# Bin results stacked in the rows of one tile, and sums sent back to tokens as a high and a low part in one product

## Chip, cores and metric

One Trainium2 chip, one core (core 0). The metric is the device time of one launch in microseconds (us); lower is better. The engines are named as the profile names them: PE (TensorE) multiplies, PEld loads its weights, DVE (VectorE), ACT (ScalarE), POOL (GpSimd), and SP, which here only issues the DMA transfers of the weight stream.

## What is computed

The reference runs 256 tokens of width 1024 through two stacked blocks. Only the two mixtures of experts matter here:

```
# first mixture: 8 experts, 1024 -> 2816 -> 1024, two experts per token
logits = ht @ router
top_vals, top_idx = lax.top_k(logits, 2)
gates = softmax(top_vals)
out = sum_e gate[:, e] * ((silu(ht @ wg[e]) * (ht @ wu[e])) @ wd[e])

# second mixture: 4 groups of 4 experts, 1024 -> 256 -> 1024,
# one group per token, two experts inside it
g_val, g_idx = lax.top_k(softmax(ht @ w_rg + b_rg), 1)
hid = silu(a) * u * combine[..., None]
out = einsum('tef,efd->td', hid, w_down)
```

With the inputs given, the router of the reference sends 25, 63, 73, 46, 66, 88, 87 and 64 tokens to the eight experts of the first mixture, and 62, 47, 92 and 55 tokens to the four groups of the second.

## The kernel before

All weights come as one stream of 1 MB chunks, read once and in order; SP issues the transfers (lines 163 and 171) as soon as one of 11 buffers comes free, five of them called raw, six of them pairs called whi and wlo. A buffer comes free when the unit of work that used it is done (`retire`). In the mixtures nothing else is loaded, so each stretch goes at the pace of the stream or at the pace of PE, whichever is slower there, with a reserve of a few chunks between them.

An expert (in the second mixture a group) works on a **bin** of up to 96 token slots. The tokens of a bin are picked by a product with a one-hot matrix (`one_hots`, `gather`). The first 64 slots are computed always. The other 32 are computed inside `tc.If(more == 1)`, a branch on PE that is taken where a bin has more than 64 tokens. More than 96 would go to a fallback (`overflow`), behind a branch of all engines after the third expert of each mixture; it isn't entered here.

Per expert the units of work come in this order: gate-up of a group of columns (`bin_unit`), the down product of the group before (`bin_down`), the turning of the newest hidden values (`turn_hid`, which calls `bin_hid`), the next gate-up, and so on. The first mixture has six groups per expert (five of 512 columns, one of 256), so six hidden values are turned per expert; the second has one unit per expert.

- `bin_unit` puts gate and up of the 64 slots side by side into two halves of the rows of one PSUM bank (64 weight columns of PE each, both products at once), and those of the 32 slots into the four quarters of a second bank.
- `bin_mul` (lines 988 to 999) makes silu(gate) * up by three ACT and three DVE instructions. Its result tile `h` holds the 64 slots in rows 64 to 127 and the 32 slots in rows 32 to 63, in other columns.
- `bin_hid` (lines 1001 to 1009) transposes `h` on PE: for each 128 columns one transpose of 64 rows (line 1005) and one of 32 (line 1007); ACT copies the result for the down product (line 1008).
- `bin_down` sums the down products of an expert or group over its units in two PSUM banks `dn`.
- `bin_y` (lines 1029 to 1035) copies the two banks to SBUF in float32: two ACT copies (1032, 1034) and one DVE copy (1033). It runs 12 times, once per expert of the first mixture and once per group of the second.
- `scatter` (lines 1037 to 1054) sends the sums back to the tokens, once per half of the tokens, inside the gate-up of a later unit. Two float32 products of 64 rows each (line 1042, called through `mm`, so at line 342 in the profile) go to two banks, and inside a branch (line 1043) four more of 64 rows and 256 columns (line 1047). DVE adds the banks to `x` (line 1052 or 1054).
- `one_hots_T` (lines 910 to 922) turns the one-hots for `scatter`: three batches of four products with the identity, each followed by an ACT copy (line 920). It runs six times, once per pair of bins.
- `last_down` (line 1079) ends each mixture: there `bin_y` and `scatter` come right behind the last down product, and the next block waits for `x`.

The order of the work is that in which this code is written; DVE and ACT take their instructions strictly in that order.

Of the kernel before, what the change touches and what calls it, by code (L numbers as in the profile page):

```python
# [18 lines left out]
P = 128  # L19
# [18 lines left out]
WIN = 288  # L38
W_A, W_B0, W_B1 = 0, 128, 160
# [205 lines left out]
def block_kernel(ctx: ExitStack, tc: tile.TileContext, stream, x_in, cst_in, cols_in, small_in, sgu_in,  # L245
# [651 lines left out]

# [12 lines left out]
    def one_hots_T(pm, p):  # L910


        got = []
        for tag, w in (("k3" if p % 2 == 0 else "sguT", W_A), (f"t{6 + p % 2}", W_B0), (f"t{4 + p % 2}", W_B1)):
# [4 lines left out]
            pt = sl(tag, [2, 2, P])  # L919
# [32 lines left out]
    def to_slots(pm, i, src, n):  # L952

        b = ps("ms")
        for j, w in enumerate((W_A, W_B1)):
            for tb in range(2):
                mm(b[:, j * n:(j + 1) * n], pm[:, tb, i, w:w + P].bitcast(F32), src(tb), tb == 0, tb == 1)
# [4 lines left out]
    def bin_unit(xT, more, n, hooks=()):  # L962
# [5 lines left out]
        for r in range(KT // kc):  # L968
            row = W.take()
            for j in range(kc):  # L970
                k, at = kc * r + j, 2 * n * j
                todo.append((k, row, at))
                for h in range(2):
                    mm(a[h * HALF:(h + 1) * HALF, 0:n], xT[:, k, 0:HALF], row[:, at + h * n:at + (h + 1) * n], k == 0,
# [3 lines left out]
        with tc.If(more == 1) as c:  # L978
            for k, row, at in todo:
                for q in range(4):  # L980
                    c0 = at + (q % 2) * n + (q // 2) * m
# [6 lines left out]
    def bin_mul(banks, n, s, h, up=None):  # L988


        m = n // 2
        for (j, c0, m, lo, w, to) in ((0, 0, n, 0, HALF, HALF), (1, n, m, 0, MORE, MORE), (1, n + m, m, HALF, MORE, MORE)):
            r = slice(lo + w, lo + 2 * w)
            t, v, b = s[r, c0:c0 + m], h[to:to + w, c0:c0 + m], banks[j]
            nc.scalar.activation(t, b[lo:lo + w, 0:m], AF.Silu)  # L995
            if up is None:
                nc.vector.tensor_mul(v, b[r, 0:m], t)  # L997
            else:
                nc.vector.scalar_tensor_tensor(v, b[r, 0:m], up[r, j], t, op0=ALU.mult, op1=ALU.mult)

    def bin_hid(h, n, hT):

        b = ps("ms")[:, 0:4 * CAP].rearrange("p (k s) -> p k s", k=4)
        for f in range(n // P):
            nc.tensor.transpose(b[:, f, 0:HALF], h[HALF:P, f * P:(f + 1) * P], ident[HALF:P, HALF:P])
        for f in range(n // P):
            nc.tensor.transpose(b[:, f, HALF:CAP], h[MORE:HALF, n + f * P:n + (f + 1) * P], ident[MORE:HALF, MORE:HALF])  # L1007
# [21 lines left out]
    def bin_y(dn):  # L1029

        y = sl("k2", [512 + T])
        nc.scalar.activation(y[0:HALF, 0:512], dn[0][0:HALF], AF.Copy)
        nc.vector.tensor_copy(y[HALF:P, 0:512], dn[0][HALF:P])
        nc.scalar.activation(y[:, 512:], dn[1][:, 0:T], AF.Copy)
        return y

    def scatter(pt, i, y, tb, more, gate=None, tag="ms"):

        bs = [ps(tag), ps(tag)]
        for h in range(2):  # L1040
            r = slice(h * HALF, (h + 1) * HALF)
            mm(bs[h], pt[0][r, i, tb], y[r, 0:512], True, True)
        with tc.If(more == 1):  # L1043
            for q in range(2):
                for h in range(2):
                    r = slice(h * HALF, (h + 1) * HALF)
# [704 lines left out]
```

## Time and profile before

| | |
|---|---|
| median of 3 runs (range) | 1530.71 us (1527.68 to 1533.65) |
| profiled execution | 1530.3 us |
| its span, first to last instruction | 1528.6 us |
| PE busy | 1467.3 us, 96% |
| DVE, ACT, POOL busy | 618.5, 507.1, 115.5 us |
| HBM read | 426.02 MB, 279 GB/s over the span |
| granted clock of PE, mean | 0.990 of full speed |

Times in views of the trace count from the start of the span. The first mixture runs from about 427 to 1137 us and the second from about 1340 to 1501 us. A busy PE is not the same as a PE at its peak: the ends of matmuls are modelled, so the distance between two starts says more than the length of one. The DMA share is that of the 16 DMA engines; it reads 1.02 where they never rest.

### The profile page before, as it was taken

Reading aid. Unit: us, or ns where it says so; the run is one execution under the profiler, and the core shown is the slowest. Engines: PE = TensorE matmul, PEld = TensorE weight load, DVE = VectorE, ACT = ScalarE, POOL = GpSimd, SP = SyncE. Lnnn points to the kernel's source line nnn. Section 1 sums busy time; section 2 is a strip of 40 time slices with the busy share of each in tenths; the row PEclk is TensorE's granted clock in tenths of the full one; section 3 lists DMA queues with packets and bytes.
Section 4 is the critical chain, followed back from the end, with each engine's and each line's share of the span. In section 5 each row is a group of like instructions: output and inputs, shape, how many; then the busy total and the mean of one; then the engine's idle time right before and its main releaser. Section 6 shows DMA issues by size and latency. Waiting matters only on the chain. (4 is left out here: it accounts for less than half of the span.)

```text
span 1528.6 us, 22736 instructions
## 1 busy us (share of the span) xinstructions
PE 1467.3 (96%) x9322; PEld 888.1 (58%) x9322; DVE 618.5 (40%) x1132; ACT 507.1 (33%) x856; POOL 115.5 (8%) x98
## 2 busy tenths in 40 slices
PE   7899999999999999989999999999989999999998
PEld 5778888877753334433444444444347888865546
DVE  6986666689621211112111110101147566732235
ACT  7645444485431111111111111111136554621134
POOL 4804000053000000000000000000002000000000
PEclk9999999999999999999999999999999999999999
DMA  8434455542499999999999978899984345388870
GB/s 324 158 117 172 170 185 217 187 163 79 161 353 414 416 412 414 414 395 366 416 413 391 385 306 340 319 368 388 406 325 150 126 165 200 138 337 299 334 273 28
DMA packets 84086, 429.03 MB, mean 281 GB/s; under 512 B 9328, under 2 KB 9840, under 8 KB 53488
## 3 DMA queue, kind: packets, MB, share of 16 engines
q1 hardware_dynamic: 83232, 425.01, 71.8%
q8 instruction: 101, 1.65, 0.4%
q10 hardware_dynamic: 720, 2.10, 0.3%
q14 instruction: 33, 0.27, 0.1%
HBM read 426.02 MB, written 1.05 MB: 279 GB/s over the span
## 5 line engine op out<-in xcount | busy, mean ns | idle before, releaser
L997 DVE TENSOR_TENSOR k<-gu,k 64x512 f32<-64x512 f32 (+1 forms) x141 | 68.0, 482 | 405.8 <-ACT k L995 405.0
L342 PE MATMUL gu<-whi,xah 128*128 128x512 f32 x528 | 180.0, 403 | 5.5 <-ACT whi L197 3.9
L198 DVE SCALAR_TENSOR_TENSOR wlo<-raw,cols,whi 128x1024 fp32r<-128x1024 f32 (+1 forms) x146 | 160.9, 1140 | 48.5 <-ACT whi L197 48.5
L995 ACT ACTIVATE k<-gu 64x512 f32<-64x512 f32 (+1 forms) x141 | 59.4, 422 | 353.4 <-PE gu L342 324.3
L342 PE MATMUL gu<-wlo,xah 128*128 128x512 f32 x528 | 174.0, 393 | 1.5 <-POOL wlo L203 1.2
L342 PE MATMUL gu<-whi,xal 128*128 128x512 f32 x528 | 173.2, 392 | 0.9 <-DVE xal L457 0.9
L197 ACT ACTIVATE whi<-raw,cols 128x1024 fp32r<-128x1024 f32 (+1 forms) x146 | 142.5, 1026 | 25.4 <-PE gu L342 15.7
L342 PE MATMUL dn<-raw,k 128*64 128x512 f32 (+1 forms) x856 | 126.7, 495 | 1.6 <-DMA raw<-in_stream_dram 1.2
L342 PEld LDWEIGHTS gu<-wlo,xah 128*128 128x128 f32 x528 | 99.8, 189 | 23.8 <-POOL wlo L203 1.7
L342 PEld LDWEIGHTS gu<-whi,xal 128*128 128x128 f32 x528 | 99.7, 189 | 22.9 <-DVE xal L457 1.5
L342 PEld LDWEIGHTS gu<-whi,xah 128*128 128x128 f32 x528 | 97.2, 190 | 27.3 <-ACT whi L197 4.8
L446 POOL TENSOR_TENSOR rcol<-rnv,mhalf 128x1 f32<-128x1 f32 x16 | 8.9, 554 | 1311.0 <-DVE rnv L445 1311.0
L342 PE MATMUL gu<-raw,xah 128*64 128x256 f32 (+3 forms) x944 | 102.4, 406 | 5.0 <-issue 4.3
L342 PE MATMUL gu<-raw,xbh 128*64 128x256 f32 (+3 forms) x800 | 97.7, 428 | 2.7 <-DMA raw<-in_stream_dram 2.3
L202 ACT ACTIVATE whi<-raw 128x1024 fp32r<-128x1024 f32 x70 | 72.5, 1056 | 36.5 <-PE gu L342 32.1
L342 PE MATMUL gu<-whiraw,xah 128*32 128x256 f32 (+3 forms) x552 | 82.8, 453 | 0.5 <-PEq L1043 0.4
L342 PEld LDWEIGHTS dn<-raw,k 128*64 128x64 f32 (+1 forms) x856 | 41.1, 124 | 71.7 <-issue 58.5
L342 PE MATMUL gu<-wloraw,xah 128*32 128x256 f32 (+3 forms) x552 | 81.5, 447 | 0.2 <-DMA wloraw<-in_stream_dram 0.2
L1008 ACT ACTIVATE k<-ms 128x384 f32<-128x384 f32 (+1 forms) x61 | 26.4, 433 | 156.0 <-PE ms L1007 155.7
L342 PE MATMUL gu<-whiraw,xbh 128*32 128x256 f32 (+2 forms) x448 | 74.0, 482 | 1.9 <-PEq L859 1.1
L342 PEld LDWEIGHTS gu<-raw,xah 128*64 128x64 f32 (+1 forms) x944 | 45.8, 123 | 49.8 <-issue 37.5
L540 DVE SCALAR_TENSOR_TENSOR dn<-k,cols,dn 128x256 f32<-128x256 f32 x188 | 74.4, 482 | 0.0
(312 smaller groups left out, 1939.1 us busy)
## 6 DMA issues: line engine op xcount, KB each, us to landing
raw<-in_stream_dram SPq DMA_DIRECT2D x238, 1024.0 KB, 8.5
whiraw<-in_stream_dram SPq DMA_DIRECT2D x164, 512.0 KB, 10.1
wloraw<-in_stream_dram SPq DMA_DIRECT2D x164, 512.0 KB, 10.2
x<-in_x_dram SPq DMA_DIRECT2D x2, 512.0 KB, 5.7
k<-in_lnrow_dram ACTq DMA_DIRECT2D x2, 512.0 KB, 7.7
cst<-in_cst_dram SPq DMA_DIRECT2D x1, 593.0 KB, 14.8
k<-in_gains_dram ACTq DMA_DIRECT2D x1, 512.0 KB, 8.0
out_dram<-k SPq DMA_DIRECT2D x2, 256.0 KB, 2.0
```

The source lines that it names most:

```text
L197: nc.scalar.activation(hi[:, c], raw[:, c], AF.Copy, scale=g)
L198: nc.vector.scalar_tensor_tensor(lo[:, c], raw[:, c], g, hi[:, c], op0=ALU.mult, op1=ALU.subtract)
L202: nc.scalar.activation(hi, raw, AF.Copy)
L342: nc.tensor.matmul(o, a, b, start=start, stop=stop)
L446: nc.gpsimd.tensor_tensor(rs(gi, tb), v, mhalf[:, :1], op=ALU.pow)
L540: nc.vector.scalar_tensor_tensor(acc[:, ct] if j == 30 else run, src, w, run, op0=ALU.mult, op1=ALU.add)
L995: nc.scalar.activation(t, b[lo:lo + w, 0:m], AF.Silu)
L997: nc.vector.tensor_mul(v, b[r, 0:m], t)
L1008: nc.scalar.activation(hT[:, 0:n // P], b[:, 0:n // P], AF.Copy)
```

## The change

The results of a bin now lie in one layout from gate-up to the tokens.

1. `bin_unit` and `bin_mul` put gate and up at other rows, so that `h` holds slots 0 to 63 in rows 0 to 63 and slots 64 to 95 in rows 64 to 95 of the same columns. `bin_hid` then needs one transpose of 96 rows per 128 columns.
2. `bin_y` splits each sum into hi (ACT, rounded to float32r) and lo (DVE, the rest) and lays them in opposite rows of one float32r tile: six ACT copies and six DVE subtractions instead of two and one.
3. `scatter` uses one product of all 128 rows per bank (hi and lo are added by it), and inside the branch one of 64 rows and 512 columns per bank instead of two of 256. The operands are float32r instead of float32.
4. The one-hots need 256 instead of 288 columns and two batches instead of three in `one_hots_T`.

```diff
--- before.py
+++ after.py
@@ -35,8 +35,8 @@
 HALF = 64
 MORE = 32
 CAP = HALF + MORE
-WIN = 288
-W_A, W_B0, W_B1 = 0, 128, 160
+WIN = 256
+W_A, W_B = 0, 128
 
 BASE_MIX = (0, 12 + N_FFN)
 BASE_FFN = 12
@@ -894,7 +894,6 @@
 
     def one_hots(posm, p):
 
-
         e0 = 2 * p
         pm = sl("xbl" if p % 2 == 0 else "xal", [2, 2, WIN], F32R)
         for tb in range(2):
@@ -909,14 +908,13 @@
 
     def one_hots_T(pm, p):
 
-
         got = []
-        for tag, w in (("k3" if p % 2 == 0 else "sguT", W_A), (f"t{6 + p % 2}", W_B0), (f"t{4 + p % 2}", W_B1)):
+        for tag, w in (("k3" if p % 2 == 0 else "sguT", W_A), (f"t{6 + p % 2}", W_B)):
             b = ps("ms")
             for i in range(2):
                 for tb in range(2):
                     mm(b[:, (2 * i + tb) * P:(2 * i + tb + 1) * P], pm[:, tb, i, w:w + P], identr, True, True)
-            pt = sl(tag, [2, 2, P])
+            pt = sl(tag, [2, 2, P], F32R)
             nc.scalar.activation(pt.rearrange("p i b t -> p (i b t)"), b, AF.Copy)
             got.append(pt)
         return got
@@ -952,7 +950,7 @@
     def to_slots(pm, i, src, n):
 
         b = ps("ms")
-        for j, w in enumerate((W_A, W_B1)):
+        for j, w in enumerate((W_A, W_B)):
             for tb in range(2):
                 mm(b[:, j * n:(j + 1) * n], pm[:, tb, i, w:w + P].bitcast(F32), src(tb), tb == 0, tb == 1)
         t = sm([2, n], f"slots{n}", bufs=4)
@@ -971,14 +969,14 @@
                 k, at = kc * r + j, 2 * n * j
                 todo.append((k, row, at))
                 for h in range(2):
-                    mm(a[h * HALF:(h + 1) * HALF, 0:n], xT[:, k, 0:HALF], row[:, at + h * n:at + (h + 1) * n], k == 0,
+                    mm(a[h * HALF:(h + 1) * HALF, 0:n], xT[:, k, 0:HALF], row[:, at + (1 - h) * n:at + (2 - h) * n], k == 0,
                        k == KT - 1)
             if r < len(hooks) and hooks[r]:
                 hooks[r]()
         with tc.If(more == 1) as c:
             for k, row, at in todo:
                 for q in range(4):
-                    c0 = at + (q % 2) * n + (q // 2) * m
+                    c0 = at + (q in (1, 2)) * n + (q // 2) * m
                     mm(b[q * MORE:(q + 1) * MORE, 0:m], xT[:, k, HALF:CAP], row[:, c0:c0 + m], k == 0, k == KT - 1)
         with c.Else():
             mm(b[:, 0:m], zeros[:, 0:P], zeros[:, 0:m], True, True)
@@ -987,24 +985,22 @@
 
     def bin_mul(banks, n, s, h, up=None):
 
-
         m = n // 2
-        for (j, c0, m, lo, w, to) in ((0, 0, n, 0, HALF, HALF), (1, n, m, 0, MORE, MORE), (1, n + m, m, HALF, MORE, MORE)):
-            r = slice(lo + w, lo + 2 * w)
-            t, v, b = s[r, c0:c0 + m], h[to:to + w, c0:c0 + m], banks[j]
-            nc.scalar.activation(t, b[lo:lo + w, 0:m], AF.Silu)
+        for j, c0, at, w, gate, r, to, lo in ((0, 0, 0, n, HALF, 0, 0, HALF), (1, 0, n, m, 0, MORE, HALF, MORE),
+                                              (1, m, n, m, 3 * MORE, 2 * MORE, HALF, MORE)):
+            q = slice(r, r + lo)
+            t, v, b = s[q, at + c0:at + c0 + w], h[to:to + lo, c0:c0 + w], banks[j]
+            nc.scalar.activation(t, b[gate:gate + lo, 0:w], AF.Silu)
             if up is None:
-                nc.vector.tensor_mul(v, b[r, 0:m], t)
+                nc.vector.tensor_mul(v, b[q, 0:w], t)
             else:
-                nc.vector.scalar_tensor_tensor(v, b[r, 0:m], up[r, j], t, op0=ALU.mult, op1=ALU.mult)
+                nc.vector.scalar_tensor_tensor(v, b[q, 0:w], up[q, j], t, op0=ALU.mult, op1=ALU.mult)
 
     def bin_hid(h, n, hT):
 
         b = ps("ms")[:, 0:4 * CAP].rearrange("p (k s) -> p k s", k=4)
         for f in range(n // P):
-            nc.tensor.transpose(b[:, f, 0:HALF], h[HALF:P, f * P:(f + 1) * P], ident[HALF:P, HALF:P])
-        for f in range(n // P):
-            nc.tensor.transpose(b[:, f, HALF:CAP], h[MORE:HALF, n + f * P:n + (f + 1) * P], ident[MORE:HALF, MORE:HALF])
+            nc.tensor.transpose(b[:, f], h[0:CAP, f * P:(f + 1) * P], ident[0:CAP, 0:CAP])
         nc.scalar.activation(hT[:, 0:n // P], b[:, 0:n // P], AF.Copy)
         return hT
 
@@ -1028,24 +1024,24 @@
 
     def bin_y(dn):
 
-        y = sl("k2", [512 + T])
-        nc.scalar.activation(y[0:HALF, 0:512], dn[0][0:HALF], AF.Copy)
-        nc.vector.tensor_copy(y[HALF:P, 0:512], dn[0][HALF:P])
-        nc.scalar.activation(y[:, 512:], dn[1][:, 0:T], AF.Copy)
-        return y
+        ya, yb = sl("k2", [D], F32R), sl("t4", [512], F32R)
+        for y, b, w, n in ((ya, dn[0], HALF, 512), (yb, dn[1], MORE, T)):
+            for q in range(P // w):
+                c = (q * n) % y.shape[1]
+                r, o, c = slice(q * w, (q + 1) * w), slice((q ^ 1) * w, ((q ^ 1) + 1) * w), slice(c, c + n)
+                nc.scalar.activation(y[r, c], b[r, 0:n], AF.Copy)
+                nc.vector.tensor_sub(y[o, c], b[r, 0:n], y[r, c])
+        return ya, yb
 
     def scatter(pt, i, y, tb, more, gate=None, tag="ms"):
 
         bs = [ps(tag), ps(tag)]
         for h in range(2):
-            r = slice(h * HALF, (h + 1) * HALF)
-            mm(bs[h], pt[0][r, i, tb], y[r, 0:512], True, True)
+            mm(bs[h], pt[0][:, i, tb], y[0][:, h * 512:(h + 1) * 512], True, True)
         with tc.If(more == 1):
-            for q in range(2):
-                for h in range(2):
-                    r = slice(h * HALF, (h + 1) * HALF)
-                    nc.tensor.matmul(bs[h][:, q * T:(q + 1) * T], pt[1 + q][r, i, tb], y[r, 512:512 + T], start=False,
-                                     stop=True, skip_group_check=True)
+            for h in range(2):
+                r = slice(h * HALF, (h + 1) * HALF)
+                nc.tensor.matmul(bs[h], pt[1][r, i, tb], y[1][r], start=False, stop=True, skip_group_check=True)
         for h in range(2):
             xh = x[:, tb, h * 512:(h + 1) * 512]
             if gate is None:
@@ -1697,8 +1693,8 @@
     cst[:, C_TRI:C_TRI + P] = i[:, None] < i[None]
     cst[:, C_ONE:C_ONE + P] = 1
     cst[:, C_IOTA:C_IOTA + P] = i[None]
-    first, others, gap = np.arange(HALF), np.arange(HALF, CAP), np.full(MORE, -7)
-    cst[:, C_SLOT:C_SLOT + WIN] = np.concatenate([first, first, others, gap, others, gap, others])[None]
+    first, others = np.arange(HALF), np.arange(HALF, CAP)
+    cst[:, C_SLOT:C_SLOT + WIN] = np.concatenate([first] * 2 + [others] * 4)[None]
     cst[:, C_CENT:C_CENT + P] = np.eye(P) - (i[:, None] // 64 == i[None] // 64) / 64.0
     cst[:, C_BLK:C_BLK + 2] = (i[:, None] // 64 == np.arange(2)[None]) / 64.0
     cst[:, C_SEL:C_SEL + 256] = i[:, None] == np.arange(256)[None] // 64
```

Three places show how the instructions of the engines change. A name such as ms_4382 is a PSUM bank or a tile with its number; "x4" stands for four such rows.

PE around the turning of a hidden tile of 256 columns and the first scatter after it, before (gu, dn and ms are PSUM banks, ident the identity, xbh the tokens of a bin, k_395 the tile of sums, k_344, t_346 and t_348 the turned one-hots):

```order
L342 MATMUL dn_4338<-zeros 128x256
L1019 UNCONDITIONAL_BRANCH
L1005 MATMUL ms_4370<-ident,k_402_4330 128x64 x2
L1007 MATMUL ms_4370<-ident,k_402_4330 128x32 x2
L342 MATMUL gu_4376<-raw_4128,xbh_3436 64x512 x4
L342 MATMUL ms_4382<-k_395_4253,k_344_3551 128x512
L342 MATMUL ms_4383<-k_395_4253,k_344_3551 128x512
L1043 COMPARE_AND_BRANCH
L1047 MATMUL ms_4382<-k_395_4253,t_346_3558 128x256
L1047 MATMUL ms_4383<-k_395_4253,t_346_3558 128x256
L1047 MATMUL ms_4382<-k_395_4253,t_348_3565 128x256
L1047 MATMUL ms_4383<-k_395_4253,t_348_3565 128x256
```

The same place after the change (k_393 and t_394 are the two tiles of sums):

```order
L342 MATMUL dn_4319<-zeros 128x256
L1015 UNCONDITIONAL_BRANCH
L1003 MATMUL ms_4351<-ident,k_401_4311 128x96 x2
L342 MATMUL gu_4355<-raw_4107,xbh_3436 64x512 x4
L342 MATMUL ms_4361<-k_393_4228,k_344_3551 128x512
L342 MATMUL ms_4362<-k_393_4228,k_344_3551 128x512
L1041 COMPARE_AND_BRANCH
L1044 MATMUL ms_4361<-t_394_4229,t_346_3558 128x512
L1044 MATMUL ms_4362<-t_394_4229,t_346_3558 128x512
```

Four transposes became two, and the branch holds two products instead of four; the place of both in PE's order is the same.

DVE at the sums of an expert, before:

```order
L997 TENSOR_TENSOR k_394_4213<-gu_4144,k_393_4212 64x512
L997 TENSOR_TENSOR k_394_4213<-gu_4145,k_393_4212 32x256 x2
L1019 UNCONDITIONAL_BRANCH
L1033 COPY k_395_4253<-dn_3660 64x512
L902 TENSOR_SCALAR xal_4268<-cst,p1posm_3406 128x288 x4
```

And after:

```order
L995 TENSOR_TENSOR k_392_4188<-gu_4119,k_391_4187 64x512
L995 TENSOR_TENSOR k_392_4188<-gu_4120,k_391_4187 32x256 x2
L1015 UNCONDITIONAL_BRANCH
L1033 TENSOR_TENSOR k_393_4228<-dn_3653,k_393_4228 64x512 x2
L1033 TENSOR_TENSOR t_394_4229<-dn_3654,t_394_4229 32x256 x4
L901 TENSOR_SCALAR xal_4249<-cst,p1posm_3406 128x256 x4
```

One copy became six subtractions, at the same place of DVE's order.

## Rows read from the trace of the kernel before

**Rows 1.** The page's first part: busy us (share), instructions.

```profile
PE 1467.3 (96%) x9322; PEld 888.1 (58%) x9322; DVE 618.5 (40%) x1132; ACT 507.1 (33%) x856; POOL 115.5 (8%) x98
```

**Rows 2.** By stretch: length, busy PE, PEld, DVE, ACT, POOL, clock, DMA share, GB/s.

```profile
427.00:455.00 28.00, 27.59 (x157) 12.50 (x158) 5.49 (x20) 8.90 (x17) 0.00 (x0) 1.00 0.88 331
455.00:580.00 125.00, 117.36 (x602) 42.24 (x602) 20.40 (x41) 20.69 (x46) 0.00 (x0) 1.00 1.02 414
580.00:690.00 110.00, 104.82 (x926) 44.33 (x920) 15.84 (x33) 14.34 (x34) 0.00 (x0) 0.98 1.02 408
690.00:715.00 25.00, 24.84 (x130) 10.12 (x128) 5.49 (x10) 3.04 (x8) 0.00 (x0) 1.00 0.87 342
...
785.00:1057.00 272.00, 271.57 (x2475) 115.68 (x2477) 36.40 (x71) 34.78 (x79) 0.00 (x0) 1.00 0.92 359
1057.00:1122.00 65.00, 63.71 (x354) 24.30 (x346) 10.67 (x20) 9.98 (x23) 0.00 (x0) 1.00 1.02 406
1122.00:1137.00 15.00, 9.88 (x29) 5.10 (x30) 8.44 (x10) 6.27 (x9) 0.00 (x0) 0.77 0.74 304
...
1390.00:1488.00 98.00, 94.43 (x891) 52.60 (x887) 26.37 (x55) 21.77 (x58) 0.00 (x0) 1.00 0.83 313
```

**Rows 3.** Waits of the DMA queue, 785 to 1057 us: us, times, longest.

```profile
SPq L171 <- PE gu L342: 73.4, 31, 9.4
```

**Rows 4.** Timeline of PE, 909 to 911 us: start, us, line, tile, count.

```profile
909.98 0.46 PE L1005 MATMUL ms<-ident,k 64*128 64x64 f32 x4
910.38 0.43 PE L1007 MATMUL ms<-ident,k 32*128 32x32 f32 x4
910.73 0.65 PE L342 MATMUL gu<-raw,xbh 128*64 128x512 f32 x2
```

**Rows 5.** Timeline of PE, 1433 to 1438 us (second mixture, group 2).

```profile
1433.44 0.33 PE L1005 MATMUL ms<-ident,t 64*128 64x64 f32 x2
...
1433.94 1.08 PE L342 MATMUL gu<-raw,xah 128*64 128x256 f32 x8
1434.95 1.13 PE L342 MATMUL ms<-k,k 64*128 64x512 f32 x4
1436.26 1.95 PE L342 MATMUL gu<-raw,xah 128*64 128x256 f32 x16 [0.18 <-PEq L1043]
```

**Rows 6.** Timeline of PE, 1504 to 1524 us: transposes of 128 rows, float32r products.

```profile
1504.51 1.03 PE L451 MATMUL ms<-ident,x 128*128 128x128 f32 x8
1505.30 0.71 PE L342 MATMUL gu<-whi,xbh 128*128 128x512 f32 x2
...
1513.56 0.39 PE L342 MATMUL gu<-whi,xbh 128*128 128x512 f32 x1
1513.79 0.39 PE L342 MATMUL gu<-wlo,xbh 128*128 128x512 f32 x1
```

**Rows 7.** Timeline of PE, 874 to 877 us: a scatter with its branch taken.

```profile
874.98 1.13 PE L342 MATMUL ms<-k,k 64*128 64x512 f32 x4
875.94 1.03 PE L1047 MATMUL ms<-k,t 64*128 64x256 f32 x8
876.90 0.65 PE L342 MATMUL gu<-whiraw,xbh 128*64 128x512 f32 x2
```

**Rows 8.** Timeline of PE, 936 to 939 us: the turning of the one-hots.

```profile
936.14 1.11 PE L342 MATMUL ms<-identr,xal 128*128 128x128 f32 x8
...
938.09 1.08 PE L342 MATMUL gu<-raw,xbh 128*64 128x512 f32 x4
```

**Rows 9.** Timeline, 1120 to 1137 us: the end of the first mixture.

```profile
1126.37 0.69 DVE L1033 COPY k<-dn 64x512 f32<-64x512 f32 x1
...
1129.32 1.41 DVE L1054 SCALAR_TENSOR_TENSOR x<-gu,G,x 128x512 f32<-128x512 f32 x2 [2.26 <-PEq L1043]
...
1131.17 2.08 PE L342 MATMUL gu<-k,sguT 64*128 64x512 f32 x4
```

**Rows 10.** Timeline, 707 to 710 us: DVE on a quarter of a bank.

```profile
708.52 0.43 DVE L997 TENSOR_TENSOR k<-gu,k 32x256 f32<-32x256 f32 x1 [0.44 <-ACT k L995]
```

## Prediction

> **What bounds the kernel now.** I read the page's busy times first, then the windows by stretch, then the waits of the DMA queue, then the timeline of PE where the change has its instructions.
>
> PE is busy for 96% of the span [rows 1], so time taken from PE's queue is what could count. But the share is an average. In the windows the reader should look at the DMA share [rows 2]: in three stretches of the first mixture, 455 to 690, 715 to 785 and 1057 to 1122 us, it is 1.02, so the transfers never rest and set the pace; there PE time that is saved is spent waiting for weights. In three others they rest: 427 to 455 (0.88), 690 to 715 (0.87) and 785 to 1057 (0.92) [rows 2]. There PE sets the pace, and the queue's longest waits are for PE to give buffers back (73.4 us in 31 waits) [rows 3]. This fits the token counts: experts 2, 4, 5 and 6 have over 64 tokens and pay for the 32 more slots; 785 to 1057 us holds 4, 5 and 6. What PE can save in a stretch before the transfers bind is their rest: (1.02 - 0.88) x 28 = 3.9 us, (1.02 - 0.87) x 25 = 3.75 us, and (1.02 - 0.92) x 272 = 27 us [rows 2]. In the second mixture they rest too (0.83 from 1390 to 1488 us, 19 us of 98) [rows 2], and PE is busy for 94.4 of 98 us, so PE's savings count there.
>
> **The change, part by part.**
>
> *Turning hidden values.* Four transposes of 64 rows and four of 32 take 910.73 - 909.98 = 0.75 us from start to start [rows 4]; two and two take 0.50 us (1433.44 to 1433.94) [rows 5]. No row shows 96 rows. Eight transposes of 128 rows take 0.79 us, 0.1 us each [rows 6], an upper end; the 64-row ones take 0.1 us each with the start-up in it, and less without, say 0.07 us, a lower end. I take 0.08 us and 0.12 us for the start-up: 0.44 us for four, 0.28 us for two. So 0.30 us are saved per tile of 512 columns and 0.22 us per tile of 256; the ends are 0.23 and 0.35 us. In experts with 64 tokens or fewer PE waits at this place for DVE's third product anyway; in the first mixture these lie mostly under the transfers, in the second I take 0.04 us for each of ten such tiles.
>
> *Scatter.* With the branch taken it takes 876.90 - 874.98 = 1.92 us; without, 1.31 us (1434.95 to 1436.26) [rows 5, 7]. A pair of 64-row float32 products of 512 columns costs 0.96 us to the next start [rows 7], for the two run side by side. A float32r product of 128 rows and 512 columns follows the next after 0.23 us (1513.56 to 1513.79) [rows 6]; two make 0.46 us. The pair of 64 rows in the branch is not shown as float32r: 0.23 us if side by side, 0.46 us if in turn; I take the middle. With 0.2 us of gaps as now, that is about 1.0 us with the branch and 0.93 us saved (ends 0.8 and 1.05), and without it 0.5 us saved at most, of which I take 0.35, since the wait for the branch (0.18 us [rows 5]) was partly covered by the longer products.
>
> The row shows where each group of products starts after a change of rows or columns in use: 0.1 us above the products' own time. [...]
>
> *One-hots.* Twelve products and three copies take 1.95 us (936.14 to 938.09) [rows 8], of which the last batch and its wait are about 0.8 us. That is saved six times, once each at about 430 us and 936 us and twice in the second mixture where PE sets the pace; DVE's 256 instead of 288 columns hide under PE.
>
> *Sums to hi and lo.* ACT has four copies more and DVE five instructions more, twelve times. By the rows the DVE part grows from one of 0.69 us to two of 0.69 and four of 0.43 us, 3.1 us in all [rows 9, 10]. The next unit on PE after it is a gate-up (its first quarter takes 1.0 us with a gap, 1433.94 to 1434.95 [rows 5], so 3.5 us or more) before the next down product needs the banks and the turned values queued on ACT behind the copies. So at ten of the twelve places I cost it at nothing; without that cover it would cost up to 2.4 us each.
>
> *The two ends.* At the end of the first mixture nothing covers it. DVE began its copy at 1126.37 us and its first addition to x at 1129.32 us [rows 9]. Now its six subtractions run from 1126.37 to about 1129.5 us and the addition follows: 0.15 us later. [...] At the end of the second mixture other products fill PE, DVE is about 1.6 us later with the first addition and the second product shorter; I take zero, between 0.7 us lost and 0.7 us won.
>
> *Sum.*
> - 427 to 455 us: the one-hots, 0.8 us (limit 3.9).
> - 580 to 715 us: six tiles of expert 2 (5 x 0.30 + 0.22 = 1.7), scatter of expert 1 (2 x 0.35) and of expert 2 (2 x 0.93) make 4.3; the transfers' rest allows 3.75. I take 3.5.
> - 785 to 1057 us: 15 tiles of 512 and two of 256 columns, 4.9; scatters of experts 4 and 5, 4 x 0.93 = 3.7; one-hots 0.8. Together 9.4 us of the 27 that the transfers leave. The scatters of experts 3 and 6 fall where the transfers bind: nothing.
> - End of the first mixture: 0.9.
> - Second mixture: four tiles of group 2, 0.9; ten others, 0.4; one-hots 1.6; scatters of groups 0 and 1, 4 x 0.35 = 1.4, of group 2, 1.9: 6.2.
>
> That is 20.8 us from the profiled execution's 1530.3 us (its span is 1528.6 us; the median of the runs is 1530.7 us): **1509.5 us**. With the other ends of the prices (tiles 1.6 us either way, scatters 1.5, ends 1.5, expert 2 up to 1) it lies between 1503.5 and 1516.
>
> **Rivals.**
>
> *The transfers take it back.* The stream rests in bursts: buffers come free only at the end of a unit. If it can't start earlier, nothing is gained from 785 to 1057 us, and 11.4 us remain: 1518.9 us. For it: the share there is already 0.92. Against: 27 us of rest stand against 9.4 us. 0.18.
>
> *The float32r product is no faster than float32.* Then two products of 128 rows, which can't run side by side, take 1.72 us where 0.86 us stood, with the branch and without. The fourteen scatters that PE's pace shows would lose 12 us and the end of the first mixture 2 us; beside tiles and one-hots that save 11 us the time would be about 1533 us, no change. Against it: the 0.23 us of the stream's own float32r products. 0.06.
>
> *The split of the sums gets in the way (slower).* If the next down product waits for the two banks, or for the turned values queued behind six ACT copies, each of the twelve places costs 2.4 us, 29 us in all: 1530.3 - 20.8 + 29 = 1538.5 us. It decides from the point where DVE's and ACT's 3.7 us (first copy 0.6, then 3.1) exceed PE's gate-up. For it: the second mixture's shortest gate-up is 3.5 us and half a microsecond of transposes before it. Against: that is only at three of the twelve places, and the first mixture's gate-ups take twice as long. 0.04.
>
> **How the numbers follow.** The forecast has 0.72. The likeliest is 1509.5 us; 1503 to 1521 us holds the forecast with its bounds and the first rival, and leaves out the other two and some unknown, about 0.2. A difference of 0.5% (7.65 us) is about what a measurement of this kernel can tell from none. Faster by more: the forecast, and most of the first rival (1518.9 is 0.77% below), 0.87. Within: the second rival and part of the first, 0.08. Slower: the third, 0.05.
>
> **What would show it.** In the changed kernel's profile: four transposes of 96 rows within 0.45 us; a scatter of about 1.0 us with the branch; a DMA share from expert 4 to 6 of 0.95 or more and that stretch some 9 us shorter; PE idle for no longer than now before the down product that follows a `bin_y`; the first mixture's end with DVE's six subtractions right ahead of the addition. I am wrong if the stretch of experts 4 to 6 is as long as before, if down products wait for DVE or ACT, or if float32r products start more than 0.3 us apart.

## The result and the profile after

The changed kernel takes 1506.47 us (median of 4 runs, 1504.53 to 1508.31) where the kernel before takes 1531.88 us (4 runs, 1527.68 to 1533.65): a ratio of 0.9845, 95% interval 0.9825 to 0.9864. The profiled execution took 1504.53 us, its span is 1502.9 us, 25.7 us less than the 1528.6 us of before.

The page of the changed kernel, first part (busy us, share, instructions), against [rows 1]:

```profile
PE 1431.9 (95%) x8990; PEld 863.9 (57%) x8990; DVE 645.4 (43%) x1192; ACT 525.0 (35%) x898; POOL 115.4 (8%) x98
```

PE lost 35 us of busy time, DVE gained 27 and ACT 18. The windows by stretch answer to [rows 2] (length, busy PE, PEld, DVE, ACT, POOL, clock, DMA share, GB/s); the bounds are moved along with the work:

```profile
426.00:455.00 29.00, 28.49 (x155) 12.12 (x154) 5.09 (x19) 8.18 (x16) 0.00 (x0) 1.00 0.89 346
455.00:580.00 125.00, 116.39 (x590) 40.26 (x592) 23.39 (x48) 22.70 (x51) 0.00 (x0) 1.00 1.02 422
580.00:669.00 89.00, 88.54 (x775) 35.76 (x771) 14.49 (x28) 13.09 (x30) 0.00 (x0) 1.00 1.02 421
...
774.00:1037.00 263.00, 263.00 (x2383) 108.53 (x2383) 40.04 (x80) 38.15 (x86) 0.00 (x0) 1.00 0.95 372
...
1102.00:1118.00 16.00, 7.31 (x20) 5.01 (x21) 10.65 (x15) 8.02 (x13) 0.00 (x0) 0.57 0.61 254
...
1458.00:1473.00 15.00, 10.02 (x39) 6.79 (x38) 11.20 (x17) 6.80 (x13) 0.00 (x0) 0.88 0.00 0
```

Three things are to be seen. Experts 4 to 6 (774 to 1037 us) are 9 us shorter with PE busy throughout. In the two stretches above in which the transfers never rest (1.02) they carry 422 and 421 GB/s, and no longer 414 and 408. And at the two ends of the mixtures, the last two kinds of row, PE is busy for 46% and 67% of the time, at a granted clock of 0.57 and 0.88 of full speed.

For the accounts below each kernel's trace is cut at the first ACT copy of each `bin_y`. "Expert 4" is the stretch from `bin_y` of expert 3 to that of expert 4, and so on; "end 1" goes from `bin_y` of expert 7 to the first instruction of POOL in the next block (line 446, the root for the scale of a token), "end 2" from `bin_y` of the last group to the same mark behind it. Expert 0 and "groups 0, 1" begin at the last such mark ahead of their mixture. Saved us against the profiled execution of before, with its lengths in the first row; the last column has the mean granted clock of PE in end 1, in groups 0 and 1 and in end 2, as a share of full speed:

| kernel | expert 0 | 1 | 2 | 3 | 4 to 6 | 7 | end 1 | groups 0, 1 | groups 2, 3 | end 2 | clock |
|---|---|---|---|---|---|---|---|---|---|---|---|
| before, us | 91.00 | 86.81 | 90.88 | 88.66 | 291.94 | 67.81 | 17.44 | 92.64 | 64.43 | 19.21 | 0.80, 0.96, 1.00 |
| before, once more | -0.06 | 0.02 | 0.00 | -0.66 | 0.00 | -1.05 | -0.62 | 1.23 | -0.01 | -0.01 | 0.72, 0.98, 1.00 |
| **changed** | 1.81 | 1.49 | 2.39 | 3.74 | 9.67 | -0.31 | -1.87 | 8.61 | 3.62 | -4.34 | 0.66, 1.00, 0.86 |
| changed, once more | 1.71 | 1.48 | 2.39 | 4.54 | 9.68 | -0.58 | -1.32 | 8.59 | 3.62 | -4.02 | 0.73, 1.00, 0.85 |
| hidden values alone | -0.12 | 0.05 | 1.53 | 0.70 | 4.60 | -0.97 | 0.17 | 3.32 | 1.65 | -1.61 | 0.80, 0.98, 0.92 |
| hidden values alone, once more | -0.05 | 0.09 | 1.53 | 0.74 | 4.61 | -0.80 | -0.53 | 1.34 | 1.65 | -1.62 | 0.72, 0.94, 0.92 |
| scatter alone | 1.64 | 1.63 | 0.86 | 0.21 | 4.96 | 1.73 | -1.91 | 5.02 | 2.33 | -3.66 | 0.66, 0.98, 0.85 |
| before, buffers moved | 0.92 | 1.46 | 0.00 | 1.91 | 0.00 | 0.42 | -0.39 | 1.28 | 0.00 | 0.00 | 0.71, 0.98, 1.00 |
| changed, buffers as before | 0.80 | -0.06 | 2.39 | 3.99 | 9.67 | -2.37 | -1.25 | 7.10 | 3.62 | -4.28 | 0.73, 0.98, 0.85 |
| changed, buffers 256 bytes on | 1.67 | 1.49 | 2.38 | 3.71 | 9.68 | 1.01 | -1.24 | 6.01 | 3.61 | -3.98 | 0.73, 0.96, 0.85 |
| changed, copies first | 1.72 | 1.49 | 2.38 | 3.64 | 9.68 | -0.97 | 0.63 | 6.03 | 4.20 | -1.00 | 0.80, 0.96, 0.92 |
| changed, copies first, once more | 1.84 | 1.49 | 2.39 | 4.47 | 9.68 | -1.11 | -0.12 | 8.59 | 4.19 | -1.02 | 0.71, 1.00, 0.92 |

The block between the mixtures stays within 0.3 us, and the part ahead of expert 0 begins or ends up to 1.7 us earlier or 1.2 us later by chance (407.67 us in before, 406.28 in the changed kernel, 408.61 in its second run). Experts 1, 2 and 4 to 6 and groups 2 and 3 repeat to 0.1 us, end 2 to 0.4 us; expert 3, expert 7 and end 1 to about 1 us. Groups 0 and 1 go with the clock at their start: the changed kernel's instructions save 8.6 us there at 1.00 and 6.0 us at 0.96, and the kernel before at 0.98 is 1.2 us shorter than at 0.96.

### The profile page after: what moved, and what is told of

Its sections match the earlier page's. It is cut to its first block, busy times and chain, and to the rows that moved or that the text cites. A ratio compares the mean times of both kernels' runs of the same rounds, so it can differ in the third digit from the quotient of the medians.

```text
span 1502.9 us, 22182 instructions
## 1 busy us (share of the span) xinstructions
PE 1431.9 (95%) x8990; PEld 863.9 (57%) x8990; DVE 645.4 (43%) x1192; ACT 525.0 (35%) x898; POOL 115.4 (8%) x98
## 3 DMA queue, kind: packets, MB, share of 16 engines
q8 instruction: 98, 1.61, 0.4%
HBM read 426.00 MB, written 1.05 MB: 284 GB/s over the span
```

## The experiments

The letters of the theories are given anew with each question.

### Both kernels again, and each half of the change alone

> The kernel before, once more, for the pace of the transfers. In the two profiles so far the stream moved 414 GB/s where it never rests before the change and 421 GB/s after it, which alone makes some 5 us over the 260 us of these stretches. Theory A (the gain is PE time saved where PE sets the pace; the difference in the stream's pace is chance of the execution): another execution of before shows a pace anywhere between 412 and 422 GB/s, and the 785 to 1057 us stretch (experts 4 to 6) is 291.9 us long again from the first bin_y of expert 3 to that of expert 6, within 1 us. Theory B (the change makes the stream itself faster): 414 GB/s again, within 1.

> The changed kernel once more. Theory A: the pace of the stream differs from 421 GB/s by some GB/s, and experts 4 to 6 take 282.3 us from bin_y to bin_y again, within 1 us. Theory B: 421 GB/s again, within 1, and the time within 1505 to 1508 us.

The kernel before took 1531.19 us and the changed one 1505.68 us, on the same chip. The paces came again: 414 GB/s in the first and 421 to 422 in the second. Experts 4 to 6 took 291.94 and 282.26 us again, as both theories had it. So the pace isn't chance, and something in the change makes the stream faster.

The first half alone leaves `bin_y`, `scatter` and the one-hots as before:

```diff
-            t, v, b = s[r, c0:c0 + m], h[to:to + w, c0:c0 + m], banks[j]
+            t, v, b = s[r, c0:c0 + m], h[to:to + w, at:at + m], banks[j]
...
-            nc.tensor.transpose(b[:, f, 0:HALF], h[HALF:P, f * P:(f + 1) * P], ident[HALF:P, HALF:P])
-        for f in range(n // P):
-            nc.tensor.transpose(b[:, f, HALF:CAP], h[MORE:HALF, n + f * P:n + (f + 1) * P], ident[MORE:HALF, MORE:HALF])
+            nc.tensor.transpose(b[:, f], h[0:CAP, f * P:(f + 1) * P], ident[0:CAP, 0:CAP])
```

> Only the new rows of the hidden tiles and the single transposes; sums and scatter as before. Theory A: 0.30 us per tile of 512 columns and 0.22 us per tile of 256 where PE sets the pace: 4.9 us in experts 4 to 6, 1.7 us around expert 2, 1.3 us in the second mixture, 8 us in all, a ratio of 0.9948. Rival (the turning is covered by DVE's product chain, so it gives nothing): ratio 1.000.

1519.61 us, ratio 0.9927 (0.9906 to 0.9949), at 414 GB/s. Theory A's 0.9948 lies at the edge of the interval, the rival's 1.000 outside it. Experts 0 and 1 gain nothing (-0.12 and 0.05 us), though PE has less to do there: the transfers bind. Experts 2 and 4 to 6 gain 1.53 us each.

The second half alone is the changed kernel with `bin_mul` and `bin_hid` laid out as before:

```diff
-            nc.tensor.transpose(b[:, f], h[0:CAP, f * P:(f + 1) * P], ident[0:CAP, 0:CAP])
+            nc.tensor.transpose(b[:, f, 0:HALF], h[HALF:P, f * P:(f + 1) * P], ident[HALF:P, HALF:P])
+        for f in range(n // P):
+            nc.tensor.transpose(b[:, f, HALF:CAP], h[MORE:HALF, n + f * P:n + (f + 1) * P], ident[MORE:HALF, MORE:HALF])
```

> The new sums, one-hots and scatter; the hidden tiles and their two transposes per 128 columns as before. Theory A: 0.8 us at the start of the first mixture, 2.6 us around expert 2, 4.5 us in experts 4 to 6, 4.9 us in the second mixture, less 1.9 us at the end of the first mixture, where the split now stands on the path: 11 us, a ratio of 0.993. Rival (all of the gain is here): ratio 0.985.

1517.03 us, ratio 0.9902 (0.9867 to 0.9937), at 422 GB/s. The faster stream comes with this half; experts 0 and 1, in which the transfers bind, are 1.6 us shorter each. Both ends of the mixtures lose with this half (-1.91 and -3.66 us). Theory A's 0.993 lies inside the interval and the rival's 0.985 outside it, but its parts came out otherwise: experts 2 and 3 gave 1.1 us instead of 2.6, the groups 7.4 (1.2 of it a smaller fall of the clock, as in the second run of before) instead of 4.9. By the medians the halves save 12.4 and 15.0 us, and the one run of the whole change 26.

### Where the faster stream comes from

This half also narrows the table of constants by 32 columns (`WIN` 288 to 256). The table lies in SBUF ahead of the weight buffers, so they all move down by 128 bytes: the first one of the raw chunks from byte 28800 of each partition to 28672, the first of the pairs from 118912 and 143488 to 118784 and 143360. An unused tile named pad sits in between, and its width sets the place of the buffers with no instruction changed:

```diff
-        cp.tile([P, 224], F32, tag="pad", name="pad")
+        cp.tile([P, 256], F32, tag="pad", name="pad")
```

This edit puts the changed kernel's buffers back to where they were. With 288 columns they lie at 28928, 119040 and 143616. The kernel before with 192 columns has them at 28672, 118784 and 143360.

> The changed kernel with 32 more columns (128 bytes per partition) in the unused pad tile, so that the weight buffers lie in SBUF at byte 28800, 118912 and 143488 as before the change, and no longer at 28672, 118784 and 143360; the input of constants in device memory keeps its new, shorter rows. Theory A, the stream's pace comes from where its buffers lie in SBUF: 414 GB/s instead of 421 where the transfers never rest, packets of 8192 bytes at a mean of about 314 ns instead of 310, experts 0 and 1 back at 91.0 and 86.8 us instead of 89.2 and 85.3, and the time 6 us (370 us of bound stretches by 1.6%) to 10 us longer than the changed kernel's 1506: 1512 to 1516 us. Theory B, it comes from the shorter rows of the input or from something else of the scatter part: 421 GB/s, 1506 us.

> The changed kernel with 64 more columns (256 bytes) in the pad tile: the weight buffers lie at 28928, 119040 and 143616, multiples of 256 bytes, of 512 no longer. Theory A with a grain of 256 bytes: 421 GB/s and 1506 us, as the changed kernel. Theory A with a coarser grain: 414 GB/s and 1512 to 1516 us. Theory B (not the place in SBUF): 421 GB/s and 1506 us.

> The kernel before with 32 columns fewer (128 bytes) in the pad tile, so that the weight buffers lie at 28672, 118784 and 143360 as in the changed kernel; nothing else differs. Theory A, the place in SBUF sets the pace: 421 GB/s instead of 414, experts 0 and 1 shorter by 1.8 and 1.5 us, in all about 6 us less than the kernel before (4 to 8): 1524 to 1528 us. Theory B: 414 GB/s and 1531 us, no difference.

The same 116 us of transfers without rest, in windows (clock, DMA share and GB/s at the end of a row). Kernel before:

```profile
459.00:575.00 116.00, 108.55 (x536) 39.24 (x533) 18.66 (x39) 19.14 (x43) 0.00 (x0) 1.00 1.02 414
```

The kernel before with its buffers moved to 28672:

```profile
459.00:575.00 116.00, 109.94 (x547) 39.73 (x547) 18.16 (x37) 18.88 (x43) 0.00 (x0) 1.00 1.02 421
```

The changed kernel with its buffers back at 28800:

```profile
459.00:575.00 116.00, 106.19 (x495) 35.72 (x491) 21.18 (x44) 20.39 (x46) 0.00 (x0) 1.00 1.02 414
```

The changed kernel with its buffers at 28928:

```profile
459.00:575.00 116.00, 107.28 (x515) 36.47 (x515) 20.34 (x42) 20.60 (x46) 0.00 (x0) 1.00 1.02 422
```

The place of the buffers sets the pace. 28672 and 28928 are multiples of 256, 28800 is half way between: a step of 128 bytes loses the pace (414 GB/s instead of 422) and one of 256 has it back (422). Nothing else of the change is needed. The kernel before with its buffers moved takes 1523.99 us, ratio 0.9956 (0.9939 to 0.9973), 6.0 us less than the 1530.01 us of before on that chip, within the 4 to 8 us expected. It gains where transfers bind (experts 0, 1, 3 and 7); experts 2 and 4 to 6 are the same to 0.00 us. Of its savings in the table, the 1.28 us of groups 0 and 1 are not the pace: the kernel before itself saves 1.23 us there in its second run, at the same clock of 0.98. The changed kernel takes 1508.99 us at 28800 and 1505.38 us at 28928. These 3.6 us are less than the 6 to 10 us that were expected. Summed over the stretches in which the transfers bind (experts 0, 1, 3 and 7), the profiles differ by 5.5 us there, and by 4.7 us between the two versions of the kernel before; experts 2 and 4 to 6, where PE sets the pace, feel nothing of it. So the place is worth about 5 us in either kernel, with about 1 us of chance in experts 3 and 7 each, and the medians' 3.6 and 6.0 us lie around it.

In the trace's packets between 460 and 575 us, those of 8192 bytes took a mean of 314.7 ns in the kernel before and 309.9 ns in the changed one, those of 4096 bytes 162.9 and 159.5 ns: 1.5% and 2.1% more with the buffers at 28800. In these 115 us, at the same busy share of 101.5%, the stream's queue moved 10138 packets in the kernel before and 10144 in the changed one at 28800, but 10354, 10373 and 10381 in the three whose buffers lie at multiples of 256. Why a packet takes longer half way between isn't shown; what these runs moved is the written side, in SBUF.

### What the ends lose

Timeline of DVE and ACT in the changed kernel at `bin_y` of expert 0 (start, us, engine, line, tiles, idle before and its releaser), ACT first:

```profile
495.47 0.59 ACT L1032 ACTIVATE k<-dn 64x512 fp32r<-64x512 f32 x1 [2.83 <-PE dn L342]
496.81 0.59 ACT L1032 ACTIVATE k<-dn 64x512 fp32r<-64x512 f32 x1 [0.75 <-DVE k L1033]
497.43 0.37 ACT L1032 ACTIVATE t<-dn 32x256 fp32r<-32x256 f32 x1
498.61 0.37 ACT L1032 ACTIVATE t<-dn 32x256 fp32r<-32x256 f32 x1 [0.81 <-DVE t L1033]
...
500.33 0.38 ACT L1032 ACTIVATE t<-dn 32x256 fp32r<-32x256 f32 x1 [0.49 <-DVE t L1033]
...
498.16 0.41 DVE L1033 TENSOR_TENSOR t<-dn,t 32x256 fp32r<-32x256 f32 x1
499.02 0.42 DVE L1033 TENSOR_TENSOR t<-dn,t 32x256 fp32r<-32x256 f32 x1 [0.44 <-ACT t L1032]
499.87 0.42 DVE L1033 TENSOR_TENSOR t<-dn,t 32x256 fp32r<-32x256 f32 x1 [0.44 <-ACT t L1032]
500.74 0.43 DVE L1033 TENSOR_TENSOR t<-dn,t 32x256 fp32r<-32x256 f32 x1 [0.44 <-ACT t L1032]
```

The engines work in turn. Each copy of a quarter waits for the subtraction of the quarter before, and each subtraction for its copy, so the chain runs from 495.47 to 501.17 us, 5.7 us. A copy doesn't need the subtraction before it for its data, but in the code it stands behind it and reads the same bank. The experiment writes all copies of a bank ahead of its subtractions:

```diff
-            for q in range(P // w):
...
-                nc.scalar.activation(y[r, c], b[r, 0:n], AF.Copy)
-                nc.vector.tensor_sub(y[o, c], b[r, 0:n], y[r, c])
+            for c, r, o in at:
+                nc.scalar.activation(y[r, c:c + n], b[r, 0:n], AF.Copy)
+            for c, r, o in at:
+                nc.vector.tensor_sub(y[o, c:c + n], b[r, 0:n], y[r, c:c + n])
```

> The changed kernel, with bin_y's ACT copies of a bank all ahead of DVE's subtractions of it in program order, instead of copy and subtraction in turn. Theory C, the two engines alternate on a bank because each copy is made to follow the subtraction that stands ahead of it: the chain of ten to twelve steps of 5.7 us gets 1.5 to 2.4 us shorter, the last stage of the second mixture shrinks from 23.5 us by 1 to 2 us and the end of the first by 1.5 us or more: 1502 to 1504 us instead of 1506. Rival D, the two engines share the bank's reads in hardware or wait for the same products: no difference, 1506 us.

1499.31 us (1497.12 to 1501.58), ratio 0.9790 (0.9774 to 0.9807): 6 us less than the changed kernel with its buffers at 28928 on the same chip (1505.38), more than the 2 to 4 us that were expected, and faster than both kernels. The groups of ACT's and DVE's instructions in the changed kernel (count, busy us and mean ns, idle before and its releasers):

```profile
L1032 ACT ACTIVATE t<-dn 32x256 fp32r<-32x256 f32 x48 | 18.0, 374 | 21.6 <-DVE t L1033 21.4
L1033 DVE TENSOR_TENSOR t<-dn,t 32x256 fp32r<-32x256 f32 x48 | 20.2, 421 | 16.2 <-ACT t L1032 15.9
```

The same with the copies first:

```profile
L1032 ACT ACTIVATE t<-dn 32x256 fp32r<-32x256 f32 x48 | 18.0, 374 | 3.4 <-PE dn L342 2.8
L1034 DVE TENSOR_TENSOR t<-dn,t 32x256 fp32r<-32x256 f32 x48 | 20.2, 420 | 4.9 <-ACT t L1032 4.3
```

The instructions take as long as before, and most of the waits are gone. So theory C holds: the copies waited because the subtractions stood ahead of them in the code. Whether the two engines could read one bank at the same time isn't shown, for with the copies first they don't either: ACT's copies of the second bank end at 1461.48 us and DVE's subtractions of it begin at 1461.68 (`bin_y` of group 3).

Experts 1, 2 and 4 to 6 are the same to 0.1 us with either order, so in these the length of the chain costs nothing. Groups 2 and 3 get 0.6 us from the new order, in each of two profiles. In the changed kernel ACT's copy of the turned values stands behind the six copies of group 2, and PE waits for it ahead of the next down product:

```profile
1437.11 0.33 ACT L1004 ACTIVATE k<-ms 128x192 f32<-128x192 f32 x1
1437.49 1.94 PE L342 MATMUL dn<-raw,k 128*64 128x512 f32 x8 [0.51 <-ACT k L1004]
```

With the copies first this wait is gone. The most is gained at the two ends: end 1 goes from -1.87 to 0.63 us and end 2 from -4.34 to -1.00 us. At end 1 part of that is the clock. DVE's first subtraction and its first addition to x in the changed kernel:

```profile
1106.19 0.68 DVE L1033 TENSOR_TENSOR k<-dn,k 64x512 fp32r<-64x512 f32 x1
...
1111.29 1.41 DVE L1050 SCALAR_TENSOR_TENSOR x<-gu,G,x 128x512 f32<-128x512 f32 x2
```

With the copies first:

```profile
1107.00 1.41 DVE L1034 TENSOR_TENSOR k<-dn,k 64x512 fp32r<-64x512 f32 x2
...
1110.21 1.41 DVE L1051 SCALAR_TENSOR_TENSOR x<-gu,G,x 128x512 f32<-128x512 f32 x2
```

The addition follows the first subtraction after 5.10 us, with the copies first after 3.21 us, and in the kernel before, where one copy stands for the subtractions, after 2.95 us [rows 9]. Each kernel repeats these to 0.01 us. What differs between runs of one kernel at end 1 comes behind them and goes with the clock (0.66 and 0.73 in the changed kernel, 0.80 and 0.71 with the copies first).

End 2 of the changed kernel, in the timeline of all engines. The last down product ends at about 1458.3 us:

```profile
1464.53 0.43 DVE L1033 TENSOR_TENSOR t<-dn,t 32x256 fp32r<-32x256 f32 x1 [0.44 <-ACT t L1032]
...
1465.71 1.28 DVE L198 SCALAR_TENSOR_TENSOR wlo<-raw,cols,whi 128x1024 fp32r<-128x1024 f32 x1 [0.75 <-ACT whi L197]
1467.02 1.28 DVE L1048 TENSOR_TENSOR x<-x,ms 128x512 f32<-128x512 f32 x2
1467.77 0.66 PE L451 MATMUL ms<-ident,x 128*128 128x128 f32 x4 [2.12 <-DVE x L1048]
...
1471.09 1.29 DVE L1048 TENSOR_TENSOR x<-x,ms 128x512 f32<-128x512 f32 x2 [0.98 <-PEq L1041]
1471.83 1.12 PE L451 MATMUL ms<-ident,x 128*128 128x128 f32 x4 [0.87 <-DVE x L1048]
```

The second addition to x begins 12.75 us after the first copy (1458.34 us). In the kernel before this is 10.44 us (1488.72 to 1499.16), with the copies first 9.83 us (1458.70 to 1468.53). The chain delays more than its own instructions there: ACT rounds weights (line 197) only behind its six copies, DVE's part of the rounding (line 198) waits for that, and the addition stands behind it. The 2.3 us that this place is later than in the kernel before hold 0.3 us of PE's clock (0.50 from 1470 to 1472 us): the last product of the second scatter starts at 1470.16 us, 0.93 us ahead of the addition, with the copies first only 0.62 us ahead. So about 2 us of the 4.34 us are the chain. The other 2.3 us are the clock: the four transposes behind the addition take 0.77 us to the next start where the kernel before needs 0.41, and the window from 1472 to 1476 us has a granted clock of 0.50.

### Whether the fall of the clock belongs to a kernel

In the kernel with the first half alone end 2 lost 1.61 us, though its chain is that of before. Its windows, around the second scatter:

```profile
1483.50:1487.50 4.00, 2.77 (x10) 0.94 (x9) 1.72 (x3) 1.57 (x3) 0.00 (x0) 1.00 0.00 0
1487.50:1491.50 4.00, 4.00 (x14) 3.23 (x13) 3.73 (x6) 2.67 (x3) 0.00 (x0) 0.58 0.00 0
```

And the kernel before at the same place:

```profile
1496.00:1500.00 4.00, 2.77 (x10) 0.94 (x9) 1.53 (x3) 1.57 (x3) 0.00 (x0) 1.00 0.02 4
1500.00:1504.00 4.00, 4.00 (x20) 3.38 (x21) 3.98 (x6) 2.68 (x3) 0.00 (x0) 1.00 0.00 0
```

PE did the same work in the same 4 us, 2.77 us busy, and then the clock of the next 4 us was 0.58 of full speed in the one and 1.00 in the other. The kernel with the first half alone and the copies-first version ran once more, unchanged.

> The kernel with the first part of the change alone, once more. In its first profile the clock of TensorE fell to 0.58 for 4 us at the end of the second mixture, after a stretch whose busy time (2.77 of 4 us) is that of the kernel before, whose clock stayed at 1.00. Theory E, the fall belongs to this kernel's order of work: it falls again and the last stage is 20.8 us again. Theory F, work at the edge falls on either side by chance: the last stage may be 19.2 us with a clock of 1.00. The time is 1517 to 1521 us by both.

> The version with bin_y's copies ahead of its subtractions, once more: 1497 to 1502 us again, in the stage table the same savings within 0.1 us in experts 1, 2 and 4 to 6, end of the first mixture 16.8 us instead of the changed kernel's 18.7 to 19.3. By theory E the last stage is 20.2 us again with a clock of 0.64 behind the second scatter; by theory F it may be 18.6 us with 1.00.

The first took 1522.54 us and lost 1.62 us at end 2 again, at a clock of 0.57. The second took 1501.09 us and lost 1.02 us there (1.00 before), with 0.74 and then 0.84 in the next windows of 4 us. The kernel before kept 19.2 us in both its profiles, and so did the one with moved buffers. So theory E holds in these runs: at end 2 the fall belongs to the kernel. The other profiles agree: the clock over end 2 was 0.85 or 0.86 in all four of the changed kernel, wherever its buffers lay. What in the order of work decides it stays open, since the 4 us ahead of the fall don't. At end 1 and at the start of the second mixture the clock differs between runs of one kernel: the copies-first version was 0.12 us longer than before at end 1 in its second run and 0.63 us shorter in its first, where 0.6 us in both were expected, at a clock of 0.71 and 0.80.

What such a fall costs can be read at the start of the second mixture, from the two profiles of the copies-first version. The second of them, then the first, and at the end the kernel before:

```profile
1340.00:1405.00 65.00, 62.25 (x543) 37.48 (x541) 21.48 (x53) 18.85 (x51) 0.00 (x0) 1.00 0.92 347
1340.00:1405.00 65.00, 62.51 (x522) 36.85 (x523) 21.17 (x52) 18.58 (x50) 0.00 (x0) 0.95 0.90 339
1340.00:1405.00 65.00, 59.56 (x375) 37.16 (x374) 18.56 (x70) 14.92 (x41) 0.00 (x0) 0.95 0.88 326
```

The same kernel saves 8.59 us in groups 0 and 1 where the clock stayed up and 6.03 us where it fell: the fall costs 2.6 us. The changed kernel (8.61 us at 1.00) and the one with its buffers 256 bytes on (6.01 us at 0.96) show the same.

## Why the prediction was right, and where not

The forecast was 20.8 us and the spans show 25.7 us. The time of 1506.5 us lies 3 us under the 1509.5 us named and inside the range. That it came out so near is partly luck, for errors of both signs met. By its steps:

**Where PE sets the pace, the terms held.** "785 to 1057 us" was to give 9.4 us, experts 4 to 6 gave 9.67. Tiles: 4.60 us by the first half alone, against 4.9. In the changed kernel's timeline of PE (start, us, line, tiles, count) these are a scatter with its branch, the transposes of four blocks, the one-hots and a scatter without its branch:

```profile
861.33 0.73 PE L342 MATMUL ms<-k,k 128*128 128x512 f32 x2
861.99 0.50 PE L1044 MATMUL ms<-t,t 64*128 64x512 f32 x2
862.43 1.08 PE L342 MATMUL gu<-whiraw,xbh 128*64 128x512 f32 x4
...
912.16 0.55 PE L1003 MATMUL ms<-ident,k 96*128 96x96 f32 x4
912.64 1.08 PE L342 MATMUL gu<-whiraw,xbh 128*64 128x512 f32 x4
...
920.01 1.11 PE L342 MATMUL ms<-identr,xal 128*128 128x128 f32 x8
921.05 1.08 PE L342 MATMUL gu<-raw,xbh 128*64 128x512 f32 x4
...
1407.61 0.73 PE L342 MATMUL ms<-k,k 128*128 128x512 f32 x2
1408.49 1.95 PE L342 MATMUL gu<-raw,xah 128*64 128x256 f32 x16
```

Four transposes take 0.48 us to the next start instead of 0.75 [rows 4], 0.27 saved against 0.30. A scatter with its branch takes 1.10 us instead of 1.92 [rows 7], 0.82 saved against 0.93; without it 0.88 instead of 1.31 [rows 5], 0.43 against 0.35. The one-hots take 1.04 us instead of 1.95 [rows 8], 0.91 against 0.8. The scatter with its branch is the one that came out 0.1 us longer: 0.66 us to the start of the branch's pair and 0.44 us from there, and no run parts these into gaps and the products' own time.

**The transfers' stretches.** "There PE time that is saved is spent waiting for weights" held: the first half alone gave experts 0 and 1 nothing. What failed is the step ahead of it, that the stream's pace stays what it was. The diff moved the buffers by 128 bytes, and I costed only the instructions. With the buffers back at 28800, expert 0 gained the 0.8 us of the one-hots as forecast and expert 1 nothing; the pace is worth 3.6 us in the changed kernel (1508.99 against 1505.38) and 6.0 us in the kernel before by the medians, and about 5 us in both by the stretches.

**Expert 2 and behind it.** 3.5 us were forecast for 580 to 715 us. At the old pace experts 2 and 3 gained 6.4 us, but expert 7 lost 2.4 us, about 4 in all, which is near the transfers' rest of 3.75 us. Both figures of expert 3 and 7 carry about 1 us of chance.

**The ends.** "Now its six subtractions run from 1126.37 to about 1129.5 us and the addition follows: 0.15 us later" is the step that failed. I added DVE's durations and took the copies as done ahead of them; the code has them in turn. From the first subtraction to the addition it is 5.10 us, 2.15 us more than before and not 0.15; with the copies first it is 3.21 us, near the forecast's 3.1. The shorter second scatter gave 0.9 us of that back: the second addition begins 3.20 us after the first (1111.29 to 1114.49 us) instead of 4.10 (1129.32 [rows 9] to 1133.42), with a granted clock of 0.50 during that scatter in both. The sum takes 0.9 us for this end; no run shows that term, and in its place the runs showed 1.2 to 1.9 us lost at end 1, the clock included. Zero became 4.3 us lost at end 2, of which about 2.3 us are the clock. With the copies first, end 1 gives 0.6 and -0.1 us in two profiles.

**The second mixture.** 6.2 us were forecast, and the groups gave 12.2 us. 2.6 us of that are the clock at its start, which fell in the kernel before and not in the changed one; at the same clock of 0.96 the changed kernel with its buffers 256 bytes on gave 9.6 us. Here the step "I take 0.04 us for each of ten such tiles" failed. The first half alone gave the groups 5.0 us at a clock of 0.98; the kernel before once more, at 0.98 too, gave 1.2 us, so the tiles are worth 3.7 us, where four at 0.22 and ten at 0.04 make 1.3. At full price, 0.22 to 0.30, fourteen tiles make 3.1 to 4.2. In groups 2 and 3 alone this half gave 1.65 us in both its profiles. The other 1 us isn't traced to a step. PE isn't kept waiting for DVE's third product at that place. The group of all 28 of these transposes in the changed kernel idles 1.6 us in all, most of it for PE's own sequencer:

```profile
L1003 PE MATMUL ms<-ident,t 96*128 96x96 f32 x28 | 5.9, 270 | 1.6 <-PEq L1015 1.1 <-DVE p2past L811 0.2
```

**`bin_y` at ten places "at nothing"** held at nearly all of them, even with a chain of 5.7 us instead of 3.7. Behind group 2 it cost 0.6 us.

**The rivals.** The transfers didn't take it back: their share in experts 4 to 6 rose to 0.95, and their longest wait is still for PE to give buffers back. Waits of the DMA queue, 774 to 1037 us in the changed kernel, against [rows 3]:

```profile
SPq L171 <- PE gu L342: 66.9, 31, 7.9
```

The float32r products are faster: two of 128 rows and the start-up take 0.66 us (861.33 to 861.99), where the pair of float32 took 0.96 [rows 7]. The split got in the way at the two ends, where nothing covered it, and in the third rival's own way at one place of the other ten: behind `bin_y` of group 2 a gate-up of 4 us (1433.05 to 1436.98 us) ends ahead of the chain, and the next down product waits 0.51 us for turned values queued behind the copies. That is far from the 2.4 us at each of twelve places.

## What to carry to other kernels

A diff that changes the size of a tile can move the tiles behind it, and a stream that binds feels where its buffers start: keep the targets of large transfers at multiples of 256 bytes (these runs tried such places, 421 to 422 GB/s, and those half way between, 414), and look at GB/s in a stretch without rest before and after. When two engines make a chain on one bank, write all of the first engine's instructions ahead of the second's (here ACT idled 21.6 us ahead of 48 copies in turn with the subtractions, and 3.4 us with the copies first), and cost the chain as it is written, not as the sum of one engine. A chain that is free inside a pipeline, where other work covers it, is paid at the pipeline's end, where here a fall of PE's clock came on top (0.57 and 0.88 over the two ends); and before a stretch is compared between two profiles, the clock in it has to be the same.

## What the runs showed of the hardware that was not expected

- Transfers into SBUF at addresses half way between multiples of 256 bytes ran at 414 GB/s, at multiples at 421 to 422 GB/s, in all eight kernels and the four repeats, over the stretch of experts 0 and 1; 8192-byte packets took a mean of 314.7 ns in the kernel before and 309.9 ns in the changed one.
- PE's granted clock was 0.58 and 0.57 of full speed for 4 us behind 4 us with 2.77 us of work in the two profiles of one kernel, and 1.00 in another behind the same work. At the start of the second mixture it was 0.95 over 65 us in one profile of a kernel and 1.00 in the other, which cost 2.6 us.
- A copy on ACT that follows a subtraction on DVE of the same bank only in the order of the code waited 0.5 to 0.8 us for it, 21.4 us over 48 copies of which every fourth had none to wait for; written ahead of the subtractions, 48 copies waited 3.4 us in all.
